# The first output projection in seven half-size products, moved behind gate B's first units, with the modulation paced by half units

## The chip, the cores and the metric

The kernel runs on one core of one Trainium2 chip. Its time is the device time of one execution in microseconds; the times below are the median of three runs, and one more execution was recorded by the hardware profiler. TensorE does the matrix products, VectorE and ScalarE the elementwise work, GpSimd (POOL) and SyncE (SP) here mostly issue transfers.

## The reference

One encoder layer over 512 tokens of width 2048, in single precision:

```python
mod = silu(c) @ w_ada + b_ada                      # shift, scale, gate: twice
h = rms_norm(x, norm1_w) * (1 + sc1) + sh1
qa, ka, va, qb, kb, vb, ga, gb = split(h @ w_in)
ya = global_gqa(rope(norm(qa)), rope(norm(ka)), va)      # 8 heads of 128
yb = neighbourhood_attention(qb, kb, vb, nat_rpb)        # 8 heads of 128
merged = sigmoid(ga) * (ya @ w_oa) + sigmoid(gb) * (yb @ w_ob)
x = x + g1 * (merged @ w_out)
h2 = rms_norm(x, norm2_w) * (1 + sc2) + sh2
x = x + g2 * ((silu(h2 @ w_ffn_gate) * (h2 @ w_ffn_up)) @ w_ffn_down)
return rms_norm(x, final_w)
```

`w_oa` and `w_ob` are 1024 x 2048, `w_out` 2048 x 2048, `w_ffn_gate` and `w_ffn_up` 2048 x 5632.

## The kernel before

**Products.** Each single-precision operand is split into a high half (a copy by ScalarE, rounded, line 163) and a low half (the difference, by VectorE, line 165). `mm3` (lines 183 to 185) makes three products of them: high x high, high x low, low x high. It reads the moving columns interleaved: of each `n` columns, one from the first half, then one from the second. So tokens come out in another order, which the host's `MERGED` and `LAST` undo.

**Units.** Weights come in units of 512 KB: `unit` (line 190) loads a `raw` tile through SP's queue, `wsplit` splits it into one `whl` tile. There are four `raw` and three `whl` buffers; where a pool `wq` is open, `buffer` gives some more of both. `form1` uses a unit's weights as the stationary side against all 512 tokens, 24 products a unit; `form2` streams the weights. After each unit both call `pump`.

**`pump`** is where other work enters the program's order: what is due in `soon`, one entry of `later`, then `pace["steps"]` steps of the generators in `bg`. One of these is the modulation: `ada_acc` adds one 128 x 1024 block of `w_ada`, scaled by `cact`, to `acc` on VectorE (line 357); the block `mw` is fetched through POOL's queue (line 335), three at a time. 112 such steps are done until the end of the output projections, 16 more during `w_out`, from SP's queue. After each 16 steps the sum is split, summed over the partitions by TensorE (`row_sum`, `row_products`) and stored.

**Order.** A scheduler lays out each engine's instructions by their order in the program and by when it expects inputs and buffers to be ready; a modulation step is pinned behind VectorE's instruction traced before it. The order of the stages after global attention (`att_a`):

- `gates(sg_b, GB, 0, 8)`: gate B's first 1024 columns, four calls of `form1` with 4 units each; `keep_gate` applies the sigmoid (line 609) and stores the tiles to memory. Modulation begins here, one step per unit.
- Two halves of neighbourhood attention: values by `form2`, then per pair of heads queries and keys by `form1` and the attention `att_b`. The attended heads are stored as `y_d`, as those of `att_a` were.
- `gates(sg_b, GB, 8, KT)`: gate B's rest, while `attended` loads and splits all 16 heads, one per pump, through SP's queue (lines 816 and 163).
- The output projections: for each pair of column blocks `form1` with `w_oa` on the heads of A, `form1` with `w_ob` on those of B, 2 units each. `gated` loads the gate (line 843; those of A that are still raw get their sigmoid here, line 845) and multiplies (line 847); the two are added (line 859) and split into `mT`. Steps per pump follow a list `paces`.
- `w_out`, residual and norm, then the feed-forward network.

**Seven products.** The feed-forward network's first two matrices use `group7`: both operands are cut into 2 x 2 blocks; with sums of blocks seven block products take the place of eight. `wforms` makes the sums of a weight's blocks on VectorE (lines 1008 to 1011) and splits them into four `whl` tiles, `xforms` does the same for the tokens' side once, and lines 1081 to 1093 put the seven results together. A product has 256 columns there. `wq` gives it one more `raw` and two more `whl`.

Of the kernel before, what the change touches and what calls it, by code (L numbers as in the profile page):

```python
# [54 lines left out]
MERGED = stream_order(T)  # L55
LAST = MERGED[stream_order(T // 2)]

# [55 lines left out]
def encoder_block(ctx: ExitStack, tc, xp, xT, c, ada1_w, ada2_w, b_ada, norm1_w, w_in, q_norm_w, k_norm_w, bias,  # L113
# [13 lines left out]
    wbufs = {"raw": 4, "w": 3, "at": 0}  # L127
    wq = None
    taken = collections.Counter()

    def buffer(tag, shape, dt, first, name=None):

        more = {"raw": 1, "whl": 2}[tag] if wq else 0
# [72 lines left out]
    pace = {"steps": 1}  # L206

    paces = []

    def pump():  # L210
        if paces:
            pace["steps"] = paces.pop(0)
# [6 lines left out]
        for _ in range(pace["steps"]):  # L219
            advance()  # L220

    def advance():
        if bg:
            try:
                next(bg[0])
            except StopIteration:
                bg.pop(0)
                advance()

    def form1(ws, c0, g, xs, banks, evac, eng=V):  # L230
# [3 lines left out]
        for k0 in range(0, n, nk):  # L234
            m = min(nk, n - k0)
            for w, bs in zip(ws, banks):
                hi, lo = wsplit(w, k0, m, c0, g * P, eng)
# [10 lines left out]
    def form2(w, c0, xs, evac, r0=0, eng=V, tiles=range(NT), tags=("mm",) * NT):  # L248
# [3 lines left out]
        for k0 in range(0, n, 2):  # L252
            m = min(2, n - k0)
            hi, lo = wsplit(w, r0 + k0, m, c0, 512, eng)
            for kk in range(m):
                xh, xl = xs[k0 + kk]
                for i in tiles:
                    sl = slice(i * P, (i + 1) * P)
                    mm3(banks[i], xh[:, sl], xl[:, sl], hi[:, kk], lo[:, kk], k0 + kk == 0, k0 + kk == n - 1, 256)
            pump()  # L260
# [297 lines left out]
    for k1 in range(1, KT + 1):  # L558
# [19 lines left out]
        for c0, accs, ends in GROUPS:  # L578
# [8 lines left out]
            for i, acc in enumerate(accs):  # L587
                sl = slice(i * P, (i + 1) * P)
                b = bank(next(turn))
                for k in range(a0, k1):  # L590
# [3 lines left out]
                    else:  # L594
                        mm3(b, wh[:, sl], wl[:, sl], hh, hl, k == a0, k == k1 - 1, T)
# [17 lines left out]
    def gates(dst, base, j0, j1, eng=V):  # L613
        for j in range(j0, j1, 2):
            form1([w_in], base + j * P, 2, hT, [[bank("mm"), bank("mm")]], keep_gate(dst[j:]), eng)


    p_a = tc.alloc_tile_pool(name="p_a", bufs=1, side="right")
    behind(nc.sync.dma_start(rp, rope.rearrange("p (i s d) -> p i s d", i=NT, s=2)))
    nw = {}  # L620
    for nm, w in (("q", q_norm_w), ("k", k_norm_w)):
        nw[nm] = small.tile([P, HD], F32, tag=f"nw{nm}", name=f"nw{nm}", bufs=1)
        nc.sync.dma_start(nw[nm], w.partition_broadcast(P).rearrange("p o d -> p (o d)"))

    def head_ssq(src, nh, acc):
        for h in range(nh):
            junk = io.tile([P, 512], F32, tag="io", name="junk")[:, :HD]
            S.activation(junk, src[:, h * HD:(h + 1) * HD], AF.Square, accum_out=acc[:, h:h + 1])

    def norm_rope(src, nh, i, r, w, dst):  # L630

        n = nh * HD
        h3 = lambda a: a[:, :n].rearrange("p (h d) -> p h d", h=nh)
        bt = lambda a: a.unsqueeze(1).to_broadcast([P, nh, a.shape[1]])
        a, b, rot = (p_a.tile([P, 512], F32, tag="rt", name="rt", bufs=3) for _ in range(3))
        for h in range(nh):
            hs = slice(h * HD, (h + 1) * HD)
            V.scalar_tensor_tensor(b[:, hs], src[:, hs], r[:, h:h + 1], w, op0=ALU.mult, op1=ALU.mult)
        V.tensor_mul(h3(a), h3(b), bt(rp[:, i, 0, :]))
        for e in range(2):  # L640
# [868 lines left out]
```

## Time and profile before

| | |
|---|---|
| runs, median (lowest, highest) | 2486.97 us (2481.64, 2489.78) |
| profiled execution, its own time | 2481.72 us |
| its span, first to last instruction | 2480.0 us |
| TensorE busy | 2449.8 us, 99% |
| VectorE busy | 1883.9 us, 76% |
| ScalarE busy | 1027.6 us, 41% |
| DMA, mean over the span | 184 GB/s |
| `w_oa` and `w_ob` products | 852.7 to 1020.5 us |

In the profile's rows, PE is TensorE, DVE is VectorE, ACT is ScalarE; `mm<-whl,h3h` is a product that writes the buffer `mm` from `whl` and `h3h`, with buffer numbers left out. A row of a group gives shapes, the count, the busy time, the mean of one in ns, and behind the second bar the idle time of its engine just before it, with what ended it. TensorE's instructions overlap, so that the time from start to start is shorter than what one lasts.

### The profile page before, as it was taken

To read this page: it belongs to the slowest core of one execution; us is meant where nothing else is said; L and a number is where in the kernel's file an instruction comes from. 1 tells how busy PE (TensorE), PEld (TensorE's weight loads), DVE (VectorE), ACT (ScalarE), POOL (GpSimd) and SP (SyncE) were. 2 spreads that over 40 slices of the span, in tenths; PEclk is the share of its full clock that TensorE was granted. 3 is DMA by queue.
4 is the path that set the end of the run, shared out by engine and by line. 5 is a ranking of instruction groups with operands and counts; after the bars stand their busy time and mean duration, and the time that the engine had idled before them with its cause. 6 is when DMAs were issued, how large, how long until landed. Compare 5 with 4: busy or idle time off the path is not lost.

```text
span 2480.0 us, 40653 instructions
## 1 busy us (share of the span) xinstructions
PE 2449.8 (99%) x16607; PEld 2270.1 (92%) x16607; DVE 1883.9 (76%) x2511; ACT 1027.6 (41%) x1424; POOL 151.0 (6%) x254
## 2 busy tenths in 40 slices
PE   8999999999999999999999999999999999999998
PEld 7888888888888888888999999999999998999997
DVE  8995776556566577566898888888888885787877
ACT  5223544224334333236744444444444454434333
POOL 0100000111011111011000000000000000000010
PEclk9999999999999999999999999999999999999999
DMA  9864234865655877676353343433433456547563
GB/s 362 296 245 156 81 102 135 273 203 184 191 187 195 300 252 264 233 266 229 111 170 117 122 130 127 136 125 112 132 128 129 135 187 227 190 141 242 192 243 127
DMA packets 217466, 457.46 MB, mean 184 GB/s; under 512 B 15056, under 2 KB 68672, under 8 KB 208832
## 3 DMA queue, kind: packets, MB, share of 16 engines
q1 hardware_dynamic: 179872, 308.19, 37.6%
q0 software_dynamic: 29728, 132.20, 15.2%
q10 hardware_dynamic: 7680, 14.48, 1.6%
q8 instruction: 130, 2.13, 0.3%
q14 instruction: 56, 0.46, 0.1%
HBM read 410.74 MB, written 44.07 MB: 183 GB/s over the span
## 4 chain that ended last, share of the span: by engine, by line
PE 82%; DVE 9%; DMA 4%; issue 2%; ACT 1%; DVEq 0%; POOL 0%; ACTq 0%; POOLq 0%
PE mm L185 18%; PE mm L184 18%; PE mm L183 17%; PE S L183 6%; PE S L184 6%; PE S L185 6%; PE Y L183 3%; PE Y L184 3%; PE Y L185 3%; DVE raw L492 2%; DVE whl L165 2%; DMA raw<-in_w_down 1%; DMA yr<-y 1%; PE T L185 1%; PE T L183 1%
## 5 line engine op out<-in xcount | busy, mean ns | idle before, releaser
L163 ACT ACTIVATE whl<-raw 128x1024 fp32r<-128x1024 f32 (+1 forms) x483 | 462.0, 960 | 758.5 <-PE mm L185 376.5
L165 DVE TENSOR_TENSOR whl<-raw,whl 128x1024 fp32r<-128x1024 f32 (+1 forms) x483 | 531.2, 1109 | 255.5 <-ACT whl L163 255.1
L165 DVE TENSOR_TENSOR whl<-ta,whl 128x1024 fp32r<-128x1024 f32 x104 | 127.2, 1223 | 66.4 <-ACT whl L163 66.4
L357 DVE SCALAR_TENSOR_TENSOR acc<-mw,cact,acc 128x1024 f32<-128x1024 f32 x124 | 158.4, 1278 | 18.8 <-DMA mw<-in_ada_w 14.0
L163 ACT ACTIVATE whl<-tb 128x1024 fp32r<-128x1024 f32 x104 | 110.4, 1061 | 149.6 <-PE S L185 120.1
L163 ACT ACTIVATE whl<-ta 128x1024 fp32r<-128x1024 f32 x104 | 110.1, 1059 | 144.8 <-PE mm L185 113.9
L165 DVE TENSOR_TENSOR whl<-tb,whl 128x1024 fp32r<-128x1024 f32 x104 | 127.0, 1221 | 4.6 <-ACT whl L163 3.6
L335 POOL DMA_DIRECT2D mw<-in_ada_w x112 | 59.8, 534 | 681.7 <-DVE acc L357 384.1
L1008 DVE TENSOR_TENSOR ta<-raw 128x512 f32<-128x512 f32 x104 | 71.8, 690 | 31.5 <-DMA raw<-in_w_down 29.3
L1009 DVE TENSOR_TENSOR ta<-raw,ta 128x512 f32<-128x512 f32 x104 | 71.6, 688 | 28.0 <-DMA raw<-in_w_down 24.9
L183 PE MATMUL mm<-x56h,whl 128*128 128x256 f32 x336 | 92.4, 275 | 0.0
L184 PE MATMUL mm<-x56l,whl 128*128 128x256 f32 x336 | 92.4, 275 | 0.0
L185 PE MATMUL mm<-x56h,whl 128*128 128x256 f32 x336 | 92.4, 275 | 0.0
L183 PE MATMUL mm<-whl,s 128*128 128x256 f32 x320 | 88.1, 275 | 0.0
L183 PE MATMUL mm<-x3h,whl 128*128 128x256 f32 x320 | 88.0, 275 | 0.0
L184 PE MATMUL mm<-x3l,whl 128*128 128x256 f32 x320 | 88.0, 275 | 0.0
L185 PE MATMUL mm<-x3h,whl 128*128 128x256 f32 x320 | 88.0, 275 | 0.0
L183 PE MATMUL S<-x56h,whl 128*128 128x256 f32 x320 | 88.0, 275 | 0.0
L184 PE MATMUL S<-x56l,whl 128*128 128x256 f32 x320 | 88.0, 275 | 0.0
L185 PE MATMUL S<-x56h,whl 128*128 128x256 f32 x320 | 88.0, 275 | 0.0
L184 PE MATMUL mm<-whl,s 128*128 128x256 f32 x320 | 88.0, 275 | 0.0
L185 PE MATMUL mm<-whl,s 128*128 128x256 f32 x320 | 88.0, 275 | 0.0
(1603 smaller groups left out, 8574.4 us busy)
## 6 DMA issues: line engine op xcount, KB each, us to landing
raw<-in_w_in SPq DMA_DIRECT2D x133, 512.0 KB, 4.4
mw<-in_ada_w POOLq DMA_DIRECT2D x112, 512.0 KB, 4.9
raw<-in_w_gate SPq DMA_DIRECT2D x92, 512.0 KB, 3.6
raw<-in_w_up SPq DMA_DIRECT2D x88, 512.0 KB, 3.6
raw<-in_w_down SPq DMA_DIRECT2D x88, 512.0 KB, 5.2
raw<-in_ada_w POOLq DMA_DIRECT2D x29, 1024.0 KB, 7.0
raw<-in_w_out SPq DMA_DIRECT2D x48, 512.0 KB, 5.1
ffd<-c SPq DMA_DIRECT2D x10, 1024.0 KB, 4.8
```

Of the source, the lines that this page charges most:

```text
L163: high = pin(S.activation(hi, src, AF.Copy))
L165: latest[:] = [high, pin(eng.tensor_sub(lo, src, hi))]
L183: nc.tensor.matmul(o, lh, rh, start=start, stop=False, **kw)
L184: nc.tensor.matmul(o, lh, rl, start=False, stop=False, **kw)
L185: nc.tensor.matmul(o, ll, rh, start=False, stop=stop, **kw)
L335: mod["queue"].dma_start(w, ada2_w[n * P:(n + 1) * P, :])
L357: behind(V.scalar_tensor_tensor(acc, part, cact[:, k:k + 1], acc, op0=ALU.mult, op1=ALU.add))
L492: V.scalar_tensor_tensor(raw, raw, 1.0, call, op0=ALU.mult, op1=ALU.mult, accum_out=y)
L1008: V.tensor_sub(t1, b12, b11)
L1009: V.tensor_sub(t2_, b22, t1)
```

## The change

`w_oa` leaves the loop of the output projections. After `att_a` a pool `p_o` is opened as `wq`, with one more `raw` and one more `whl`. Two calls of `form1` for gate B follow; in their pumps `yforms` loads the eight heads of A from memory and makes their seven forms. Then four times `merged_a`: it fetches a quarter of gate A, applies the sigmoid where it is still raw, calls `group7` with `w_oa` (two units, K = 1024), multiplies by the gate and stores the quarter as `ma_d`. After the second and third of them comes one more call of `form1` for gate B each. `group7`, `wforms` and their helpers move up in the file with no other change.

`gates(sg_b, GB, 8, KT)` then reads only B's eight heads. The last loop does `w_ob` alone and loads A's part from `ma_d`.

The modulation's generators go to a list of their own, `mods`. They start with neighbourhood attention, and `slot`, called twice per unit (after half of its products and after `pump`), makes a step when `pace["rate"]` has added up to one: 0.8 in the values, 0.75 in queries and keys, 0.65 in gate B's rest, 0.95 in the first five turns of the `w_ob` loop, none in the last three and in the first pass of `w_out`, then 0.5. `row_products` come after one pump more. All `mm3` outside global attention's scores interleave by 256 columns instead of 512, so that the seven products' order is that of everything they meet.

```diff
-MERGED = stream_order(T)
-LAST = MERGED[stream_order(T // 2)]
+MERGED = stream_order(T // 2)
+LAST = MERGED[MERGED]
...
+    def slot():
+        pace["due"] += pace["rate"]
+        if pace["due"] >= 1 and (fetched or mod["next"] < mod["end"]):
+            pace["due"] -= 1
+            advance(mods)
...
         if later:
             later.pop(0)()
-        for _ in range(pace["steps"]):
-            advance()
+        advance(bg)
+        slot()
...
-                        mm3(bs[j], hi[:, kk, sl], lo[:, kk, sl], xh, xl, k0 + kk == 0, k0 + kk == n - 1, T)
+                        mm3(bs[j], hi[:, kk, sl], lo[:, kk, sl], xh, xl, k0 + kk == 0, k0 + kk == n - 1, 256)
+                    if kk == m // 2 - 1:
+                        slot()
                 pump()
...
-        soon.append((1, lambda: row_products(hl, tag, dst, then)))
+        soon.append((2, lambda: row_products(hl, tag, dst, then)))
...
     p_a.release()
     p_q.release()
+    wq = tc.alloc_tile_pool(name="p_o", bufs=1, side="right", reuse_waits="tile")
+    more_buffers(1, 1)
...
+    def yforms(s):
+        e, o = (raw_tile("ye") for _ in range(2))
+        for a, r in enumerate((e, o)):
+            for q in range(2):
+                nc.sync.dma_start(half(r)[:, :, q], y_d[4 * s + 2 * a + q].rearrange("p (t n) -> p t n", t=2))
...
+        V.tensor_add(sa[:, :512], a21, a22)
+        V.tensor_sub(sa[:, 512:], sa[:, :512], a11)
+        V.tensor_sub(sb[:, :512], a11, a21)
+        V.tensor_sub(sb[:, 512:], a12, sa[:, 512:])
...
+            split(*hl, src)
...
+    def merged_a(n):
+        c, g = (wq.tile([P, 2048], F32, tag=t, name=t, bufs=1) for t in "cg")
+        v, gv = quarters(c), quarters(g)
+        for f in range(4):
+            nc.gpsimd.dma_start(gv[:, f // 2, :, f % 2], sg_a[4 * n + f].rearrange("p (t n) -> p t n", t=2))
+        if n < 3:
+            S.activation(g, g, AF.Sigmoid)
+        group7(lambda s: wforms(w_oa, 4 * s, n * 512), ya, (0, 1), ((v[:, 0, 0], v[:, 1, 0]), (v[:, 0, 1], v[:, 1, 1])))
+        for a in range(2):
+            sl = slice(a * 1024, (a + 1) * 1024)
+            V.tensor_mul(c[:, sl], c[:, sl], g[:, sl])
+        nc.gpsimd.dma_start(ma_d[n], c)
+
+    for s in range(2):
+        later.extend([lambda: None, functools.partial(yforms, s), lambda: None, lambda: None])
+    gates(sg_b, GB, 0, 4)
+    for n in range(4):
+        merged_a(n)
+        if n in (1, 2):
+            gates(sg_b, GB, 2 * n + 2, 2 * n + 4)
+    wq.release()
+    wq = None
+    more_buffers(0, 0)
     p_w = tc.alloc_tile_pool(name="p_w", bufs=1, side="right")
     mod["pool"] = p_w
-    bg.extend(ada_mod(k, (s2, b_sc2, n2, t2, b_sh2)) for k in range(0, KT, 4))
+    mods.extend(ada_mod(k, (s2, b_sc2, n2, t2, b_sh2)) for k in range(0, KT, 4))
...
-    gates(sg_b, GB, 0, 8)
+    fetch()
...
+        pace["rate"] = 0.8
+        form2(w_in, VB + hh * 512, hT, lambda i, b: split(*v[i], b))
+        pace["rate"] = 0.75
...
-    later.extend(functools.partial(attended, h) for h in range(KT))
+    later.extend(functools.partial(attended, h) for h in range(8))
+    pace["rate"] = 0.65
     gates(sg_b, GB, 8, KT)
...
-            if any(src[j] is t for t in sg_a[:12]):
-                S.activation(g, g, AF.Sigmoid)
...
-    paces.extend([2, 1, 1, 1, 1, 1, 1] * 4 + [0] * 4 + [0] * 2 + [1] * 16)
     for j in range(0, KT, 2):
+        pace["rate"] = 0.95 if j < 10 else 0.0
         ma, mb = [], []
-        for w, ys, sg, to in ((w_oa, yT[:8], sg_a, ma), (w_ob, yT[8:], sg_b, mb)):
-            tag = next(turn)
-            form1([w], j * P, 2, ys, [[bank(tag), bank(tag)]], gated(sg[j:], to))
+        for e in range(2):
+            ma.append(p_y.tile([P, T], F32, tag="ma", name="ma", bufs=4))
+            a, q = divmod((j + e) % 4, 2)
+            nc.sync.dma_start(ma[e].rearrange("p (t n) -> p t n", t=2), quarters(ma_d[j // 4])[:, a, :, q])
+        tag = next(turn)
+        form1([w_ob], j * P, 2, yT, [[bank(tag), bank(tag)]], gated(sg_b[j:], mb))
...
     for cc in range(2):
         w_out_pass(cc, range(NT))
+        pace["rate"] = 0.5
```

More of the change, by code (lines that the diff above doesn't have):

```diff
@@ L611, in keep_gate, with gates @@
         return evac
-    def gates(dst, base, j0, j1, eng=V):
+    def gates(dst, base, j0, j1):
         for j in range(j0, j1, 2):
[L615 to L623, printed above, removed]
@@ L810, in encoder_block @@
[L810 to L821 removed]
+            form1([w_in], base + j * P, 2, hT, [[bank("mm"), bank("mm")]], keep_gate(dst[j:]))
     def half(t, n=2):
@@ L866, in encoder_block @@
-    p_y.release()
-    p_w.release()
-    aside.release()
-    taken.update({t: -1 - taken[t] for t in ("raw", "whl")})
-    wq = tc.alloc_tile_pool(name="wq", bufs=1, side="right", reuse_waits="tile")
-    x2_d = dram.tile([T, D], F32, name="x2d")
-    p_w = tc.alloc_tile_pool(name="p_w2", bufs=1, side="left", reuse_waits="tile")
-    mod.update(pool=p_w, queue=nc.sync, end=128)
-    p_r = tc.alloc_tile_pool(name="p_r", bufs=1, side="right", reuse_waits="tile")
-    gate = p_r.tile([P, D], F32, name="gate1")
@@ new lines, in values @@
+    def values():
+        for i in range(NT):
+            v = st(F32R)
+            vA.append((v[:, :256], v[:, 256:]))
+            split(*vA[i], kv[i][:, 256:])
+            if i % 2:
+                yield
+    vA = []
+    q = pair(p_a, "q", 4 * T, 1)
+    bg.extend([normed(kv, 2, nw["k"], kT), normed(q_acc, 4, nw["q"], q), values()])
+    q1 = [st(F32) for _ in range(NT)]
+    form2(w_in, QA + 512, hT, lambda i, b: S.activation(q1[i], b, AF.Copy))
+    flush()
+    y_d = [dram.tile([P, T], F32, name=f"y{h}") for h in range(16)]
@@ new lines, in encoder_block, with attended, __init__, __getitem__ @@
+    p_b.release()
+    p_y = tc.alloc_tile_pool(name="p_y", bufs=1, side="right", reuse_waits="tile")
+    yT = [pair(p_y, f"y{k}", T, 1) for k in range(8)]
+    def attended(h):
+        yr = raw_tile("yr")[:, :T]
+        nc.sync.dma_start(yr, y_d[8 + h])
+        split(*yT[h], yr)
+    later.extend(functools.partial(attended, h) for h in range(8))
+    pace["rate"] = 0.65
+    gates(sg_b, GB, 8, KT)
+    p_h.release()
+    class Tokens:
+        def __init__(self, t):
+            self.t = t
+        def __getitem__(self, ix):
+            t, c = divmod(ix[1].start // P, 2)
+            return self.t[:, t, c * P:(c + 1) * P]
@@ new lines, in encoder_block, with gated, evac @@
+    p_m = tc.alloc_tile_pool(name="p_m", bufs=1, side="left")
+    mx = [pair(p_m, f"m{j}", 1024, 1) for j in range(KT // 2)]
+    mT = [tuple(Tokens(half(t)[:, :, k % 2]) for t in mx[k // 2]) for k in range(KT)]
+    def gated(src, dst):
+        def evac(w, j, b):
+            g = io.tile([P, T], F32, tag="io", name="g")
+            nc.sync.dma_start(g, src[j])
+            o = p_y.tile([P, T], F32, tag="o", name="o", bufs=4)
+            V.tensor_mul(o, g, b)
+            dst.append(o)
+        return evac
@@ new lines, in encoder_block @@
+    p_y.release()
+    p_w.release()
+    aside.release()
+    more_buffers(1, 2)
+    wq = tc.alloc_tile_pool(name="wq", bufs=1, side="right", reuse_waits="tile")
+    x2_d = dram.tile([T, D], F32, name="x2d")
+    p_w = tc.alloc_tile_pool(name="p_w2", bufs=1, side="left", reuse_waits="tile")
+    mod.update(pool=p_w, queue=nc.sync, end=128)
+    p_r = tc.alloc_tile_pool(name="p_r", bufs=1, side="right", reuse_waits="tile")
+    gate = p_r.tile([P, D], F32, name="gate1")
+    xc = {cc: p_r.tile([P, NT, 512], F32, tag=f"x{cc}", name=f"x{cc}") for cc in (3, 2)}
@@ new lines, in encoder_block, with load_x @@
+    xn = [None, None, xc[2], p_r.tile([P, NT, 512], F32, tag="n3", name="n3")]
+    xc.update({cc: p_r.tile([P, NT, 512], F32, tag=f"x{cc}", name=f"x{cc}") for cc in (0, 1)})
+    xn[:2] = xc[0], xc[1]
+    sq2 = [small.tile([P, 4], F32, tag=f"sq{i}", name=f"sq{i}", bufs=1) for i in range(NT)]
+    x3d = xp.rearrange("(i p) d -> p i d", p=P)
+    def load_x(cc):
+        if cc == 0:
+            rows(gate, g1_d)
+        nc.sync.dma_start(xc[cc], x3d[:, :, cc * 512:(cc + 1) * 512])
+    for cc in range(4):
+        later.extend([lambda: None] * (2 if cc == 0 else 3))
+        later.append(functools.partial(load_x, cc))
```

541 lines of the change are left out of this document (253 added, 288 removed).

## The prediction

> **What bounds the kernel now.** I read the page's totals and chain first, then the table of stretches, then the waits of the stages that the change touches, last the rows that carry a duration.
>
> ```profile
> span 2480.0 us, 40653 instructions
> PE 2449.8 (99%) x16607; PEld 2270.1 (92%) x16607; DVE 1883.9 (76%) x2511; ACT 1027.6 (41%) x1424; POOL 151.0 (6%) x254
> PE 82%; DVE 9%; DMA 4%; issue 2%; ACT 1%; DVEq 0%; POOL 0%; ACTq 0%; POOLq 0%
> ```
>
> TensorE is busy for 99% of the span and makes up 82% of the chain of waits. So time goes away only where TensorE gets fewer products, or where it now stands idle. The table of stretches shows both (columns: stretch, length, busy us and count by engine, granted clock, DMA share, GB/s). The first five rows are the stages: gate B's first four units with the end of attention A, neighbourhood attention, gate B's last units, the two output projections, and the start of `w_out`.
>
> ```profile
> 400.00:480.00 80.00, 79.68 (x390) 68.39 (x389) 44.25 (x49) 25.50 (x36) 11.12 (x21) 1.00 0.75 254
> 480.00:780.00 300.00, 298.90 (x1481) 256.61 (x1480) 182.64 (x257) 108.11 (x198) 34.29 (x61) 1.00 0.57 182
> 780.00:853.00 73.00, 71.31 (x328) 61.42 (x328) 49.45 (x53) 28.59 (x38) 13.59 (x24) 1.00 0.94 326
> 853.00:1020.00 167.00, 167.00 (x775) 146.12 (x774) 113.61 (x128) 49.74 (x61) 18.93 (x35) 1.00 0.71 240
> 1020.00:1120.00 100.00, 100.00 (x465) 87.49 (x464) 61.64 (x60) 30.99 (x43) 15.21 (x13) 1.00 0.80 272
> 880.00:980.00 100.00, 100.00 (x465) 87.50 (x464) 78.22 (x86) 29.94 (x38) 14.87 (x29) 1.00 0.83 284
> 1250.00:2000.00 750.00, 750.00 (x6719) 750.00 (x6718) 647.80 (x807) 331.31 (x351) 0.00 (x0) 1.00 0.40 128
> 780.00:800.00 20.00, 20.00 (x94) 17.46 (x94) 14.55 (x16) 8.48 (x12) 5.16 (x9) 1.00 0.98 344
> ```
>
> TensorE's idle time from 400 to 1120 us is 0.32 + 1.10 + 1.69 = 3.1 us. That is all that a better order of the work can win there.
>
> **The products of w_oa.** One wide and one narrow product last:
>
> ```profile
> L183 PE MATMUL mm<-whl,a 128*128 128x512 f32 x48 | 18.2, 379 | 0.0
> L183 PE MATMUL mm<-x56h,whl 128*128 128x256 f32 x336 | 92.4, 275 | 0.0
> ```
>
> They overlap, so I count starts. Between 880 and 980 us TensorE runs 512-column products only. 465 of them touch the 100 us, some 463 begin there: 0.216 us from start to start. From 1250 to 2000 us it runs the feed-forward network's 256-column products: 6719 touch 750 us, 0.1117 us each. Before, `w_oa` takes 8 k-blocks x 16 column blocks x 3 = 384 wide products, 384 x 0.216 = 82.9 us. After, it takes 4 groups x 2 units x 7 products x 4 pieces x 3 = 672 narrow ones, 672 x 0.1117 = 75.1 us. **Gain 7.9 us**, not the 10.4 us that an eighth of 82.9 would be, since two narrow products take 0.223 us against 0.216.
>
> The Trainium skill (TensorE: Matmul & The Clock Gate, Back-to-back issue gap) gives an isolated warm product N / 2.4 + 2.5 ns: 215.8 for 512 columns, 109.2 for 256. The wide rows agree; for the narrow ones the trace has 111.7 and decides. By the rule the gain would be 9.5 us.
>
> All other products stay: interleaving tokens over 256 instead of 512 changes addresses, not counts, and the feed-forward rows already use that form. I take 0 for it.
>
> **Gate B's last units, 780 to 853 us.** TensorE loses 1.69 us here. It waits for split weights:
>
> ```profile
> PE mm L185 <- DVE whl L165: 1.6, 2, 0.9
> ```
>
> The split that ended the first of these waits, and ScalarE's queue in front of it:
>
> ```profile
> 819.83 1.22 DVE L165 TENSOR_TENSOR whl<-raw,whl 128x1024 fp32r<-128x1024 f32 x1
> ```
>
> ```profile
> 816.12 0.63 ACT L845 ACTIVATE g<-g 128x512 f32<-128x512 f32 x1 [3.23 <-DMA g<-sga]
> 822.16 0.63 ACT L845 ACTIVATE g<-g 128x512 f32<-128x512 f32 x1 [2.73 <-DMA g<-sga]
> 823.43 0.63 ACT L163 ACTIVATE y12h<-yr 128x512 fp32r<-128x512 f32 x1 [0.65 <-DMA yr<-y]
> ```
>
> ScalarE stands before gate A's sigmoid and before attended heads, whose loads are late at a DMA share of 0.94; the weight's high half is queued behind. The change removes both from this queue: gate A is not loaded here, and 8 heads are read instead of 16. Against that the modulation rises from one step per unit to 1.3. In bytes per unit of 24 x 0.216 = 5.18 us: half a head less, 0.13 MB, and 0.3 steps of 512 KB more, 0.16 MB. So DMA stays as full, but ScalarE no longer waits at its head for sigmoid loads. Bounds 0 and -1.7; I take **-1.4 us**.
>
> **Where modulation starts.** Its first fetch waits for memory of the pool before it:
>
> ```profile
> DVE acc L355 <- DMA mw<-in_ada_w: 7.0, 1, 7.0
> ```
>
> ```profile
> 419.28 0.75 DVE L355 TENSOR_SCALAR acc<-mw,cact 128x1024 f32<-128x1024 f32 x1 [7.00 <-DMA mw<-in_ada_w]
> ...
> 425.35 1.29 DVE L357 SCALAR_TENSOR_TENSOR acc<-mw,cact,acc 128x1024 f32<-128x1024 f32 x1 [1.01 <-DMA mw<-in_ada_w]
> 426.56 1.22 DVE L165 TENSOR_TENSOR whl<-raw,whl 128x1024 fp32r<-128x1024 f32 x1
> ```
>
> VectorE stands 7 us, and the next weight split comes behind four steps, at 426.56; TensorE loses 0.32 us in that stretch. This leaves the first stage (-0.3) and returns at neighbourhood attention. There the memory is that of the new pool, whose last user is the 1 MB store of a merged group: a load of that size lands in 4.8 us.
>
> ```profile
> ffd<-c SPq DMA_DIRECT2D x10, 1024.0 KB, 4.8
> ```
>
> The wait may grow to 12 us, but weights have three buffers, two 5.18 us units ahead. Bounds 0 and +2; **+0.5**.
>
> **The new stage.** Attention A's heads are read and split there, and VectorE makes sums. Its durations from the same code in the feed-forward network:
>
> ```profile
> L165 DVE TENSOR_TENSOR whl<-ta,whl 128x1024 fp32r<-128x1024 f32 x81 | 99.1, 1224 | 58.3 <-ACT whl L163 58.3
> L165 DVE TENSOR_TENSOR whl<-tb,whl 128x1024 fp32r<-128x1024 f32 x81 | 98.9, 1221 | 0.9
> L1008 DVE TENSOR_TENSOR ta<-raw 128x512 f32<-128x512 f32 x82 | 56.6, 690 | 2.1
> L1182 DVE TENSOR_TENSOR c<-c 128x1024 f32<-128x1024 f32 x20 | 23.5, 1220 | 0.0
> L1083 DVE TENSOR_TENSOR c<-mm,p 128x512 f32<-128x512 f32 x19 | 13.1, 692 | 21.6 <-PE mm L185 21.6
> ```
>
> A unit costs VectorE four sums (2.8), a half split (0.7, a sum's width) and three full ones (3.7): 7.1 us. A group is two units, seven sums of products (4.8) and two multiplications (2.4): 21.4 us. TensorE needs 168 x 0.1117 = 18.8 us for it. So a group alone is VectorE's by 2.6 us. But gates lie between: four calls of four units, 20.7 us each of TensorE against four splits, 4.9 us, of VectorE. The stage has 158 us of TensorE and 4 x 21.4 + 4 x 4.9 + 14 for the heads' forms = 119 us of VectorE, no modulation. Only the first two groups stand back to back, and the forms of their first unit are made during the gates. In the feed-forward network VectorE has 647.8 of 750 us and TensorE waits for nothing. Bounds 0 and 4 x 2.6 = 10.4; nearest is the feed-forward row; **+0.5**. ScalarE's wide sigmoids and the copies of the first product lie beside this (it has 41% of the span); ScalarE holds nothing up that TensorE waits for. SP issues 8 head loads between weight loads, POOL 16 quarter gates and 4 stores, while no modulation fetch is on POOL; row sums that come one pump later have no reader near.
>
> **Neighbourhood attention** gets 73 steps (by counting slots: 25 in the values, 48 in queries and keys) instead of 46.
>
> ```profile
> L357 DVE SCALAR_TENSOR_TENSOR acc<-mw,cact,acc 128x1024 f32<-128x1024 f32 x46 | 58.7, 1276 | 0.0
> ```
>
> ```profile
> L335 POOL DMA_DIRECT2D mw<-in_ada_w x112: 527/528/641, 412.6 to 975.8; - x112
> DMA to landing us min/median/max: 3.1/4.9/8.9
> ```
>
> 27 x 1.28 = 35 us more of VectorE in 300, from 183 to 217, and 14 MB more, from 182 to 229 GB/s: both have room. POOL issues each fetch in 0.53 us. What is queued behind a step is the next split, which its three buffers let run up to two units ahead. **+0.3 us** (0 to 1.1, a doubling of the idle time there).
>
> **The w_ob loop** is the tightest place. Eighteen steps fall into its first ten units, 1.8 per unit. Rows of the stage today:
>
> ```profile
> L165 DVE TENSOR_TENSOR whl<-raw,whl 128x1024 fp32r<-128x1024 f32 x32 | 39.1, 1221 | 37.4 <-ACT whl L163 37.4
> L847 DVE TENSOR_TENSOR o<-g,mm 128x512 f32<-128x512 f32 x21 | 13.7, 683 | 9.2 <-PE mm L185 9.2
> L859 DVE TENSOR_TENSOR o<-o 128x512 f32<-128x512 f32 x14 | 9.0, 685 | 0.0
> ...
> L165 DVE TENSOR_TENSOR m5l<-o,m5h 128x512 fp32r<-128x512 f32 x2 | 1.3, 686 | 0.0
> ```
>
> ```profile
> mw<-in_ada_w POOLq DMA_DIRECT2D x26, 512.0 KB, 5.7
> raw<-in_w_ob SPq DMA_DIRECT2D x14, 512.0 KB, 4.2
> ...
> g<-sgb SPq DMA_DIRECT2D x15, 256.0 KB, 4.9
> ```
>
> Per unit: split 1.22, product by gate 0.68, sum 0.69, low half 0.69, modulation 1.8 x 1.28 = 2.30: 5.58 us of VectorE against 5.18. Over ten units it falls back 4 us. Per unit DMA brings 0.52 MB of weights, two tiles of 0.26, and 1.5 fetches (three are there already) of 0.52: 1.83 MB, 354 GB/s, where the row at 780 shows 344 at a share of 0.98. What covers this: splits lead by up to two units, and ScalarE loses the sigmoid loads that today hold weights back (the 37.4 above). Low bound 0 (this stretch has no idle now at 284 GB/s), high bound 4.5 (1.83 MB at the 326 GB/s of 780 to 853 takes 5.63 us, ten times 0.45); **+1.5**. Then `w_out`: one slot left over makes a step in its first unit, fifteen more follow from the second pass. Some fall on half-size units of 2.6 us, where split and step take 2.5. Five weight buffers cover eight such units: 0 (0 to 2).
>
> **The sum:** -7.9 - 1.4 - 0.3 + 0.5 + 0.5 + 0.3 + 1.5 = **-6.8 us**. The profiled execution took 2481.72 us (span 2480.0 and 1.7 around it), which is the low edge of the runs (2481.64 to 2489.78). The three runs and it have a mean of 2485.0; 6.8 off that is 2478.2, off the median 2480.2. I predict **2479.2 us**.
>
> **Rivals.** *The w_ob loop is paced by memory:* steps wait for fetches, splits stand behind the steps, TensorE pays 4.5 plus VectorE's 1 to 2 that lead doesn't cover. For it: 354 over 344. Against: 0.83 share costs nothing now. It gives 2479.2 + 4.5 = 2484. The Trainium skill (DMA: Bandwidth & Descriptors, Specifications) has about 358 GB/s from HBM per core; by that the loop would just fit.
>
> *All idle goes:* none of the small terms comes and all 1.7 us at gate B's end return: -7.9 - 1.7 - 0.3 = -9.9, 2476. Against it: VectorE's 5.58.
>
> *The new stage starves TensorE (slower):* four weight buffers, not the five of the feed-forward network, and sums of a finished group queued on VectorE ahead of the next unit's forms. Then each group pays its 2.6 us and the start of its forms, four sums and a half split, 3.5: 4 x 6.1 = 24 us, 2503. It decides once forms come less than 3.5 us before their use. Against: gates of 20.7 us between groups.
>
> *It doesn't do what it says:* were narrow products no cheaper in sum, nothing would be left; 6719 of them say otherwise. No chance of its own.
>
> **Chances.** A measurement here tells 0.3%, 7.5 us, from no change. Forecast 0.46 (2475 to 2482; a little over half of it is faster by more than 0.3%), all idle goes 0.18 (faster), memory paces 0.23 (within), starved 0.12 (slower), rest 0.01. So faster 0.44, same 0.43, slower 0.13. Range 2472 to 2490: below for all idle gone and the spread of runs, above for memory pacing with a stall in the new stage; the starved case is left out.
>
> **What would show it.** Right: some 384 fewer 512-column products and 672 more narrow ones between 400 and 570 us without idle TensorE; the stretch of gate B's last units without its 1.7 us. Wrong: waits of TensorE for `whl` in the w_ob loop with VectorE standing for `mw`, or in the groups of the new stage with VectorE full. The prediction fails if either exceeds 5 us.

## The result and the profile after

The changed kernel is slower: 2517.65 us at the median of six runs (2509.90 to 2522.36), against 2485.26 for the kernel before (2481.64 to 2489.78, six runs). The ratio is 1.0129, 95% interval 1.0109 to 1.0149. The forecast of 2479.2 us and its range up to 2490 were wrong, on the wrong side. One run of all that are told of here, of e9 below, took 9090.1 us; without it e9's median is 2481.21 us and not 2481.27, and why it took so long isn't known.

The totals of the changed kernel's profiled execution, whose own time is 2509.90 us, the lowest of its runs:

```profile
span 2508.0 us, 41404 instructions
PE 2451.8 (98%) x16895; PEld 2276.0 (91%) x16895; DVE 1945.2 (78%) x2587; ACT 1044.7 (42%) x1435; POOL 165.4 (7%) x274
```

TensorE has 288 more instructions (672 - 384), as forecast. The span is 28 us longer: TensorE is idle for 26 us more (56.2 against 30.2) and busy for 2 us more (2451.8 against 2449.8), though its products should take 7.9 us less. The table of stretches says where (columns as in the prediction; the third number from the end is the granted clock):

```profile
395.00:420.00 25.00, 16.49 (x86) 12.64 (x85) 19.36 (x32) 16.08 (x26) 2.88 (x4) 0.86 0.48 146
420.00:480.00 60.00, 60.00 (x416) 56.43 (x415) 42.96 (x52) 26.10 (x29) 2.68 (x4) 1.00 0.48 157
480.00:575.00 95.00, 93.06 (x618) 86.17 (x618) 60.28 (x71) 33.06 (x35) 8.07 (x12) 1.00 0.53 179
600.00:640.00 40.00, 32.64 (x142) 27.97 (x141) 27.15 (x27) 8.94 (x14) 7.41 (x14) 0.91 0.86 284
870.00:955.00 85.00, 80.39 (x381) 68.10 (x380) 56.46 (x68) 30.05 (x47) 17.65 (x31) 1.00 0.87 309
955.00:1040.00 85.00, 81.33 (x369) 70.47 (x368) 64.90 (x77) 26.32 (x34) 7.86 (x15) 0.98 0.81 265
```

These are, in order: the end of attention A; the first two groups of seven products; the other two with gate B's units between them; the end of the first values of neighbourhood attention; gate B's rest; the `w_ob` loop. TensorE is idle for 8.5, 0, 1.9, 7.4, 4.6 and 3.7 us in them, 26.1 in all; another 3.5 us lie between 640 and 870 us. Three of the rows have a granted clock below 1: an estimate from these rows of what this cost the products is 0.14 x 25 + 0.09 x 40 + 0.02 x 85 = 8.8 us. With it the busy time comes out: -7.9 + 8.8 = +0.9, near the +2.0 measured. What TensorE waited for from 380 to 1040 us (in total, times, longest):

```profile
PE mm L187 <- DVE vl L169: 8.0, 2, 7.4
PE mm L187 <- ACT whl L167: 6.5, 2, 5.2
PE mm L189 <- DVE whl L169: 4.0, 5, 2.3
PE S L189 <- DVE whl L169: 3.7, 1, 3.7
PE S L188 <- DVE kl L169: 2.1, 3, 1.6
PE mm L187 <- ACT go L625: 1.6, 1, 1.6
```

**The end of attention A.** SP's queue in the kernel before, and then in the changed kernel (start, how long the issues span, what, how many):

```profile
331.31 96.86 SPq L190 DMA_DIRECT2D raw<-in_w_in  x10
```

```profile
330.33 0.37 SPq L194 DMA_DIRECT2D raw<-in_w_in  x1
348.10 4.39 SPq L893 DMA_DIRECT2D ye<-y  x4
356.13 55.99 SPq L194 DMA_DIRECT2D raw<-in_w_in  x4
```

The last line joins loads that lie far apart. Two of its four are issued by 361.7 us:

```profile
356.13 5.55 SPq L194 DMA_DIRECT2D raw<-in_w_in  x2
```

The heads of A are loaded at 348 us, while attention A still runs, and into the `raw` buffers that weights use. Their sums can be made only when attention A's memory is free. VectorE and ScalarE there:

```profile
409.23 0.69 DVE L897 TENSOR_TENSOR sa<-ye 128x512 f32<-128x512 f32 x1 [1.58 <-PE Y L189]
```

```profile
413.33 4.10 ACT L167 ACTIVATE whl<-raw 128x1024 fp32r<-128x1024 f32 x4
```

The two `ye` tiles wait from 348 to 409 us for the last products of attention A (`PE Y`). From 330 to 412 us the weights of gate B get five loads. Two of those weights are issued by 361.7 us and yet are split only at 413.33: ScalarE has the splits of the heads ahead of them. So attention A's last steps, short products with softmax between them, run with no products of gate B to fill the gaps: 86 products in the first of the stretches. Then TensorE waits 5.2 us for the first weight. The heads thus hold gate B up in two ways: they keep buffers, and they stand ahead of its splits. No run separates the two: e1 below puts a weight ahead of the heads in both.

**The first values.** POOL, VectorE and ScalarE of the changed kernel:

```profile
572.85 0.56 POOL L920 DMA_DIRECT2D mad<-c  x1 [28.50 <-DVE c L919]
577.78 1.59 POOL L351 DMA_DIRECT2D mw<-in_ada_w  x3 [4.37 <-DMA mad<-c]
```

```profile
584.36 0.75 DVE L371 TENSOR_SCALAR acc<-mw,cact 128x1024 f32<-128x1024 f32 x1 [3.68 <-DMA mw<-in_ada_w]
...
608.79 1.28 DVE L373 SCALAR_TENSOR_TENSOR acc<-mw,cact,acc 128x1024 f32<-128x1024 f32 x1 [2.49 <-DMA mw<-in_ada_w]
...
614.78 1.28 DVE L373 SCALAR_TENSOR_TENSOR acc<-mw,cact,acc 128x1024 f32<-128x1024 f32 x1
615.98 2.48 DVE L169 TENSOR_TENSOR vl<-mm,vh 128x512 fp32r<-128x512 f32 x4
```

```profile
607.45 2.54 ACT L167 ACTIVATE vh<-mm 128x512 fp32r<-128x512 f32 x4 [2.18 <-PE mm L189]
```

The last group's store lands, the first three blocks are fetched, and the first step runs at 584.36. The program's order wants 0.8 steps per half unit of 2.6 us, one in 3.2 us, from the first unit on; here they come late, in a row, and wait for their blocks. The four values leave ScalarE at 607.45, but on VectorE their low halves stand behind the steps that are not done yet, and start at 615.98. They hold four result banks, so TensorE cannot begin the next products: 7.4 us.

### The profile page after: what moved, and what is told of

It is laid out like the page before. It is cut to its first block, busy times and chain, and to the rows that moved or that the text cites. A ratio compares the mean times of both kernels' runs of the same rounds, so it can differ in the third digit from the quotient of the medians.

```text
span 2508.0 us, 41404 instructions
## 1 busy us (share of the span) xinstructions
PE 2451.8 (98%) x16895; PEld 2276.0 (91%) x16895; DVE 1945.2 (78%) x2587; ACT 1044.7 (42%) x1435; POOL 165.4 (7%) x274
## 4 chain that ended last, share of the span: by engine, by line
PE 75%; DVE 11%; issue 7%; DMA 4%; ACT 1%; POOL 1%; SPq 0%; DVEq 0%; POOLq 0%; ACTq 0%
PE mm L187 15%; PE mm L188 15%; PE mm L189 15%; PE S L189 5%; PE S L187 5%; PE S L188 5%; PE Y L187 3%; PE Y L188 3%; PE Y L189 3%; DVE raw L508 3%; DVE whl L169 2%; DMA mw<-in_ada_w 2%; DVE acc L373 1%; PE T L189 1%; PE T L188 1%
## 5 line engine op out<-in xcount | busy, mean ns | idle before, releaser
L169 DVE TENSOR_TENSOR whl<-ta,whl 128x1024 fp32r<-128x1024 f32 x112 | 137.2, 1225 | 88.0 <-ACT whl L167 88.0
L167 ACT ACTIVATE whl<-ta 128x1024 fp32r<-128x1024 f32 x112 | 118.5, 1058 | 159.1 <-PE mm L189 120.6
L167 ACT ACTIVATE whl<-tb 128x1024 fp32r<-128x1024 f32 x112 | 118.7, 1060 | 158.2 <-PE S L189 122.1
L169 DVE TENSOR_TENSOR whl<-tb,whl 128x1024 fp32r<-128x1024 f32 x112 | 136.8, 1222 | 17.0 <-ACT whl L167 15.9
L678 DVE TENSOR_TENSOR ta<-raw 128x512 f32<-128x512 f32 x112 | 77.4, 691 | 37.7 <-DMA raw<-in_w_down 25.1
L679 DVE TENSOR_TENSOR ta<-raw,ta 128x512 f32<-128x512 f32 x112 | 77.2, 690 | 29.4 <-DMA raw<-in_w_down 24.2
```

Of the source, the lines that this page charges most:

```text
L167: high = pin(S.activation(hi, src, AF.Copy))
L169: latest[:] = [high, pin(eng.tensor_sub(lo, src, hi))]
L678: V.tensor_sub(t1, b12, b11)
L679: V.tensor_sub(t2_, b22, t1)
```

## The experiments

In all diffs the left side is the changed kernel, or the one that is named. "Before" is run beside each; on these chips it took 2487 to 2489 us.

### Head forms later (e1)

```diff
-        later.extend([lambda: None, functools.partial(yforms, s), lambda: None, lambda: None])
+        later.extend([lambda: None] * (4 if s == 0 else 1) + [functools.partial(yforms, s)])
+    later.append(lambda: None)
```

> The changed kernel with the forms of A's heads three pumps later: the first after the fifth unit of gate B, the second after the seventh. Theory 'held buffers': the two head loads take two of the four raw weight buffers from 348 us on and cannot give them back before attention A ends, so gate B's units cannot be split during attention A and TensorE has nothing to fill that attention's waits with (about 15 us of idle and slowed products between 390 and 420 us against some 3 before). Then TensorE's products from gate B go on through attention A, the stretch from 395 to 420 us gets back most of its 8.5 us of TensorE idle time, and the time falls by 8 to 13 us, to about 2507 us. Rival 'the new pool's memory': what gate B's units wait for is the extra weight buffers laid over attention A's memory; then later forms change nothing: 2514 to 2521 us.

2504.82 us (2502.06 to 2509.33), ratio 1.0072 (1.0057 to 1.0087): 12.8 us less than the changed kernel. The same stretch and the first wait of this kernel:

```profile
395.00:420.00 25.00, 24.32 (x137) 19.87 (x136) 18.68 (x31) 16.41 (x27) 2.88 (x4) 1.00 0.44 136
```

```profile
PE mm L187 <- DVE vl L169: 8.8, 1, 8.8
```

The idle time of attention A's end goes from 8.5 to 0.7 us, and the granted clock from 0.86 to 1.00; by these rows that is 7.8 and 3.5 us of the 12.8. The wait for the values stays. SP's and ScalarE's queues of e1 show that not only the buffers matter:

```profile
356.15 7.45 SPq L893 DMA_DIRECT2D ye<-y  x4
```

```profile
365.07 1.05 ACT L167 ACTIVATE whl<-raw 128x1024 fp32r<-128x1024 f32 x1
```

Two `ye` tiles are still loaded early here and first read at 407.87 us, so they stand full for over 50 us, and the idle time is gone even so. What is new is that a weight of gate B is split at 365.07, before attention A's last steps, where the changed kernel splits none until 413.33. So held buffers alone don't make this loss; the order on ScalarE and VectorE counts as well.

### First values without steps (e2)

```diff
-        pace["rate"] = 0.8
+        pace["rate"] = 0.8 if hh else 0.0
...
-        pace["rate"] = 0.75
+        pace["rate"] = 0.95
```

> The changed kernel with no modulation step in the first half's values and 0.95 instead of 0.75 per slot in queries and keys, the same number of steps in all. Theory 'steps ahead of the values' split': the 7.4 us wait of TensorE at the end of the first values comes from modulation steps that stand on VectorE ahead of the split of the values, late because their first fetch waits for the memory of the pool before. Then that wait goes, queries and keys pay 1 to 3 us more, and the time falls by 6 to 10 us, to about 2510 us. Rival 'too many steps wherever they are': the same wait appears at the next split from a bank, of queries or keys: 2514 to 2521 us.

2502.37 us (2499.82 to 2505.22), ratio 1.0061 (1.0046 to 1.0076): 15.3 us less than the changed kernel, more than expected. The wait for `vl` falls from 8.0 to 0.3 us. The steps return elsewhere in part: the waits for `kl` rise from 2.1 to 4.1 us in all, and one of 2.4 us for the split of a row sum appears. Of the gain only 4.6 us stands between the two profiled executions (spans 2508.0 and 2503.4): the changed kernel's is the lowest of its six runs, e2's the highest of its own.

### The new pacing in the kernel before (e3)

`w_oa` stays as it was; only `mods`, `slot`, the later start and row products that come one pump later come in, with a rate of 0.475 in the loop, which has twice the units:

```diff
+    gates(sg_b, GB, 0, 8)
     p_w = tc.alloc_tile_pool(name="p_w", bufs=1, side="right")
...
-    bg.extend(ada_mod(k, (s2, b_sc2, n2, t2, b_sh2)) for k in range(0, KT, 4))
+    mods.extend(ada_mod(k, (s2, b_sc2, n2, t2, b_sh2)) for k in range(0, KT, 4))
...
-    gates(sg_b, GB, 0, 8)
+    fetch()
```

> The kernel before with the new pacing alone: modulation by slots of half units, from neighbourhood attention on, with the rates of the change, and half the rate in the loop of the output projections, which is twice as long here (w_oa stays in it with its 384 wide products). Theory 'two separate losses': the pacing costs what the changed kernel shows from 600 us on, 9 at the values, 3 at gate B's rest, 2 elsewhere, and perhaps nothing in the longer loop: 2496 to 2503 us. Rival 'the pacing is harmless and the new stage's memory and order make it late': within 4 us of the kernel before, 2481 to 2490 us.

2497.24 us (2494.45 to 2498.47), ratio 1.0038 (1.0023 to 1.0053). The pacing loses 10 us by itself. But its largest wait is another one, at gate B's rest (831 us), where the products of a row sum wait in TensorE's order for a split:

```profile
PE T L382 <- ACT acch L163: 5.5, 1, 5.5
PE S L184 <- DVE kl L165: 2.8, 3, 2.3
```

The wait for `vl` is 0.2 us here, though the values have the same rate of 0.8 and the same three `mw` buffers. The difference is when the first blocks are fetched and so how soon `vl` gets its turn on VectorE:

```profile
412.94 1.08 POOL L343 DMA_DIRECT2D mw<-in_ada_w  x2 [251.30 <-PE Y L185]
```

```profile
519.39 2.63 DVE L165 TENSOR_TENSOR vl<-mm,vh 128x512 fp32r<-128x512 f32 x4 [0.36 <-ACT vh L163]
```

The blocks are asked for long before the first values, the steps ahead of the low halves aren't late, and these follow ScalarE within 0.36 us.

### No modulation (e4, e6)

120 of the 128 steps are left out, so that the modulation's sums are not computed: once in the changed kernel, once with the late head forms.

```diff
-            fetch()
-            part = fetched.popleft()
...
+            if k == 0:
+                part = mod["pool"].tile([P, 1024], F32, tag="mw", name="mw", bufs=3)
+                mod["queue"].dma_start(part, ada2_w[mod["next"] * P:(mod["next"] + 1) * P, :])
...
+            mod["next"] += 1
```

> The changed kernel with 120 of the 128 modulation steps left out: of each sum only the first block is fetched and scaled, so modulation comes out incomplete; slots, row sums and everything else stay. Theory 'two separate losses': what is left is the gain of 7.9 us in products, the loss of some 11 us at the end of attention A and 2 in the new stage, less the idle time that modulation costs in either kernel (3 us before): 2485 + 11 + 2 - 7.9 - 3 = 2487, between 2482 and 2494 us. Rival 'modulation is the whole of it': 2474 to 2479 us. Rival 'the new stage itself is slow': above 2495 us.

2491.23 us (2484.16 to 2492.59), ratio 1.0011 (1.0001 to 1.0022).

> The kernel with late head forms, with 120 of the 128 modulation steps left out (only the first block of each sum is fetched and scaled). Both losses that were found are then away. Theory: 2491 for the changed kernel without modulation less the 12.4 us of late head forms, 2478 to 2481 us, which is the kernel before less the 7.9 us of products. Rival 'the new stage eats the gain': 2484 to 2490 us.

2480.95 us (2477.17 to 2484.41), ratio 0.9966 (0.9954 to 0.9978). Without any modulation, the early head forms still cost 10.3 us (2491.23 against 2480.95): the two losses have separate causes. I first read the 7.4 us to the kernel before as the products' gain. That was wrong, as the next runs show.

### The kernel before without modulation (e9, e11, e12)

The text of e9 names a wrong count: here too 120 of the 128 steps are left out.

> The kernel before with 104 of its 112 + 16 modulation steps' worth of fetches and sums left out in the same way as in the two runs without modulation (only the first step of each sixteen is done, so the modulation sums are wrong). It tells what the 7.4 us are by which the late kernel without modulation was under the kernel before. Theory (seven products gain about 7.5 us, and the kernel before hides its modulation): 2485 to 2488 us, the same as the kernel before. Rival (the modulation costs the kernel before several microseconds, and the late kernel without it was faster only for lacking it, the products giving little): 2479 to 2483 us.

2481.27 us, ratio 0.9967 (0.9954 to 0.9979). This is the rival: the kernel before pays for its modulation as well, 7.9 us at the median. So e6 had gained nothing that could be seen. The pair was then run on one chip:

> The kernel before without its modulation steps (120 of the 128 are left out, the first of each sixteen stays; the modulation sums are wrong), next to the late kernel without them on one chip and in one set of rounds: apart they came out equal, 0.9967 and 0.9966 of the kernel before. Theory (seven products save 7.8 us of TensorE's time, the new stage gives 4 us of it back in short waits that the profiles show between 400 and 520 us): this one 2480 to 2483 us, the late one 2 to 5 us below it. Rival (nothing of the saving arrives): the two within 1.5 us. Rival (all of it arrives and the earlier equality was the chips): 6 to 8 us between them.

> The late kernel without its modulation steps (120 of the 128 are left out; the sums are wrong), the other of the pair. Theory (saving less the new stage's waits): 2 to 5 us below the kernel before without modulation. Rival (nothing arrives): within 1.5 us of it. Rival (all arrives): 6 to 8 us below it.

2480.97 us (ratio 0.9975, 0.9965 to 0.9986) for the kernel before without modulation, 2477.95 (0.9958, 0.9944 to 0.9971) for the late one: 3.0 us between the medians. The theory's 2 to 5 is met by the medians, while the intervals overlap. The profiles show one part of what is missing from the 7.9. From 395 to 575 us, first the kernel before without modulation, then the late one, then the late one's waits from 380 to 1120:

```profile
395.00:575.00 180.00, 180.00 (x880) 156.19 (x881) 67.32 (x97) 60.37 (x90) 5.80 (x10) 1.00 0.41 128
```

```profile
395.00:575.00 180.00, 176.75 (x1167) 161.85 (x1166) 124.24 (x159) 76.25 (x93) 15.22 (x23) 1.00 0.53 177
```

```profile
PE mm L187 <- ACT go L626: 1.7, 1, 1.7
...
PE mm L189 <- DVE whl L169: 0.9, 1, 0.9
```

The late kernel idles 3.25 us where the old order idles 0: 0.68 of it before 420 us, at attention A's end, and 2.57 in the new stage. That would leave 7.9 - 3.25 = 4.6 us, but over the whole span the two profiles show no gain: 2478.5 and 2479.0 us. TensorE is busy for 2448.4 and 2444.2 us, which is 4.2 less and not 7.9, and idle for 4.7 more. The late one's profiled execution is among the longest of its runs, so this doesn't settle it either. How much of the 7.9 arrives isn't shown; 3.0 us at the median is the best figure here. The largest of the stage's waits is for `go`, and ScalarE's queue of the late one tells why:

```profile
499.51 1.91 ACT L916 ACTIVATE g<-g 128x2048 f32<-128x2048 f32 x1 [10.21 <-DMA g<-sga]
...
502.28 0.57 ACT L626 ACTIVATE go<-mm 128x512 f32<-128x512 f32 x1
```

ScalarE stands 10.21 us before the sigmoid of a quarter of gate A, whose load isn't there. Behind it wait a weight's split and the two copies that free gate B's banks, and a group needs seven banks.

### An earlier first fetch (e5)

Late head forms, and the modulation's pool waits for single tiles of the pool before it, not for all of it:

```diff
-    p_w = tc.alloc_tile_pool(name="p_w", bufs=1, side="right")
+    p_w = tc.alloc_tile_pool(name="p_w", bufs=1, side="right", reuse_waits="tile")
```

> The kernel with late head forms (2504.8 us), and the modulation's pool waiting for each tile it lies over instead of for the whole pool before it; VectorE's order of instructions is the same. Theory 'late start': the steps ahead of the first values' split are late because their first fetch waits for the last store of the new stage, some 6 us after the values begin. Then the fetch leaves 4 to 8 us earlier, the 8.8 us wait of TensorE for the values' split falls below 4, and the time to 2496 to 2501 us. Rival 'fetch rate': fifteen steps in the 41 us of the values need one fetch in 2.7 us, three in flight, and come late however early they begin: 2502 to 2507 us.

2502.02 us (2497.94 to 2508.52), ratio 1.0055 (1.0035 to 1.0075), against 2504.82 in e1. The first block is asked for right behind the store, but the next two only 4.1 us later, and the longest wait for `vl` is still 5.6 us (8.8 in e1). The intervals of the two ratios overlap, so a gain isn't clear. Only part of the late start is gone, and only part of the wait. The rate of the fetches, three in flight, isn't enough by itself to make the wait: e3 has the same rate and the same three buffers, but its first blocks come some 60 us ahead, and it waits 0.2 us. What fits e1, e3 and e5 is that the late start makes the backlog, and that three buffers can't make it up before the values' evacuation. A run with a fourth `mw` buffer wasn't made.

### Late forms and quiet values (e8), an even spread (e7), evacuation first (e10)

e8 has the edits of e1 and e2 together.

> Late head forms and quiet first values together. If the two losses are separate places they add: 2517.65 - 12.8 - 15.3 = 2489.5 us, 2486 to 2493. If they share a cause (slack handed from one to the other), less: 2495 to 2502 us.

2491.71 us (2487.82 to 2498.85), ratio 1.0018 (1.0005 to 1.0031). They take 25.9 us off the changed kernel, one by one 12.8 and 15.3: they add up but for 2 us. This is the best version with modulation, and not faster than the kernel before.

e7 has the late forms, no steps in the first values, lower rates up to `w_out` but for queries and keys (0.8 for 0.75), and 32 steps instead of 16 in `w_out`:

```diff
-    mod = {"pool": None, "queue": nc.gpsimd, "next": 0, "end": 112}
+    mod = {"pool": None, "queue": nc.gpsimd, "next": 0, "end": 96}
...
+        pace["rate"] = 0.6 if hh else 0.0
...
+        pace["rate"] = 0.8
...
+    pace["rate"] = 0.55
...
+        pace["rate"] = 0.9 if j < 10 else 0.0
...
+    pace["rate"] = 0.625
...
+        pace["rate"] = 0.375
```

> Late head forms; 96 modulation steps instead of 112 before w_out and 32 in it; none in the first values, 0.8 per slot in queries and keys, 0.6 in the second values, 0.55 in gate B's rest, 0.9 in five turns of the w_ob loop, 0.625 and 0.375 in w_out. Theory 'density': fewer steps per unit of every stage that lost time leave TensorE waiting less than 8 us for modulation in all: 2479 to 2486 us, at or below the kernel before. Rival 'the order, not the density': steps pinned ahead of the splits of keys and gates cost 10 us or more wherever they are: 2488 to 2496 us.

2502.28 us (2498.21 to 2503.24), ratio 1.0050 (1.0035 to 1.0065): a miss for both. The idle time of neighbourhood attention (575 to 870 us) shrank from 10.9 us in the changed kernel to 3.1, the `w_ob` loop still loses 4.4, and `w_out` took on another loss:

```profile
1100.00:1200.00 100.00, 93.31 (x426) 79.32 (x426) 76.94 (x87) 56.55 (x85) 16.26 (x13) 0.97 0.76 249
```

6.7 us are idle from 1100 to 1200, with no wait over 1.9 us. e10 is e8 with the last half step and pump of a product put behind its evacuation (the same in `form2`):

```diff
-                    if kk == m // 2 - 1:
+                    if kk == m // 2 - 1 and k0 + m < n:
                         slot()
-                pump()
+                if k0 + m < n:
+                    pump()
         for wi, bs in enumerate(banks):
             for j in range(g):
                 evac(wi, j, bs[j])
+        for _ in ws:
+            slot()
+            pump()
```

> The kernel with late head forms and quiet first values, with one thing more: the half step and the pump of a product's last weight unit come after the product's evacuation in the program's order, so that modulation steps pinned behind it no longer stand ahead of the splits of queries, keys, values and of the gates' products. Theory (what is left of the loss is mostly the order on VectorE ahead of evacuations, like the 3.5 us wait for the keys' split): 2486 to 2490 us, the wait for kl gone. Rival (the steps' fetches and the weight splits behind them keep their cost wherever the steps stand): 2490 to 2496 us.

2497.83 us (2493.68 to 2501.91), ratio 1.0032 (1.0020 to 1.0045). The intervals of e8 and e10 overlap, so whether it is worse isn't settled; better it is not. The waits of e8, then of e10 (both up to 1180 us):

```profile
PE S L188 <- DVE kl L169: 3.5, 1, 3.5
PE mm L187 <- ACT whl L167: 3.3, 3, 2.0
```

```profile
PE mm L187 <- ACT whl L167: 4.5, 5, 2.7
...
PE T L397 <- DVE accl L169: 2.0, 1, 2.0
PE T L397 <- ACT acch L167: 1.9, 1, 1.9
```

The wait for `kl` is gone, as wanted, and its time came back as waits for weights and for the splits of a row sum. That is the rival's case.

## Why the prediction was wrong, step by step

**Where the 32 us come from**, by the runs. The early head forms cost 10.3 us (e4 to e6) to 12.8 (e1). The steps in the first values cost 15.3 (e2; 13.1 from e1 to e8). What remains above the kernel before is 3.3 us (e8). If the products with their stage give the -3.0 of e11 and e12, modulation costs some 6 us more in the later stages than it did before; that is a remainder, which no run measures. 12.8 + 13.1 + 3.3 is the way from the changed kernel over e1 and e8 to e8's kernel before (2488.4 us), so it must add up to that distance, 29.3 us. Beside its own runs of before, on another chip, the changed kernel lies 32.4 us over; the 3 us between are not explained.

**The products, -7.9: right in the price of one; the sum isn't shown.** Narrow products of a group follow each other as in the feed-forward network. In the late kernel without modulation the 1st and the 57th of a row of them start (56 x 0.1118 us apart):

```profile
504.79 0.28 PE L188 MATMUL mm<-y05l,whl 128*128 128x256 f32 x1
...
511.05 0.28 PE L187 MATMUL mm<-y12h,whl 128*128 128x256 f32 x1
```

How much of the 7.9 us reaches the end of the kernel stays open (e11, e12).

**The granted clock: not in the sum, some +8.8 us.** I took TensorE's busy time to fall by what the products save. It rose by 2.0 us, since the products ran at a granted clock of 0.86, 0.91 and 0.98 in three of the stretches; by the estimate above that costs 8.8 us. The long wait in each of them is one of the next points, so part of what e1 and e2 win is this.

**The new stage, +0.5: too small, 2.6 in e12, 1.9 in the changed kernel.** I had VectorE's sums as its danger; they cost 0.9 us at most (`whl` from VectorE). The sentence that failed is "ScalarE holds nothing up that TensorE waits for": the sigmoid on a late load stood at the head of ScalarE's queue, the very pattern that I had read in the profile of before and taken as removed. The rival with a starved stage, 24 us, was far off.

**The first stage, -0.3: the largest thing overlooked, +10 to +13.** I counted the eight head loads as issues between weight loads. I didn't ask how long each tile keeps a buffer, nor what stands behind the heads' splits. Two of the `raw` tiles stood full for 61 us, waiting for memory that attention A still used, and two of gate B's weights, asked for by 361.7 us, stood unsplit behind the heads. That the early forms cost the time is shown by e1 and by e4 with e6; which of the two ways it goes is not, and e1, with two tiles full for 52 us and no idle time, speaks for the second. And I named no work that fills attention A's gaps, though in the kernel before it was gate B's products.

**The start of modulation, +0.5 with bounds 0 and +2: +13 to +15 with the steps behind it.** "The wait may grow to 12 us" was right: the last multiplication ends at 572.5, the first step starts at 584.4. But the cover that I named, three weight buffers, covers only the next weight split. Behind the same steps stood the evacuation of four banks, which has no lead at all: the banks are needed at once. The step that failed is that only a weight's split stands behind a late step. I took it here with "weights have three buffers", and said it in the part on neighbourhood attention: "what is queued behind a step is the next split". It failed there for `kl` as well (2.1 us).

**Gate B's last units, -1.4: wrong sign, +3.** TensorE idles 4.6 us in the stretch, 1.69 before. ScalarE in the changed kernel:

```profile
903.26 1.06 ACT L167 ACTIVATE whl<-raw 128x1024 fp32r<-128x1024 f32 x1 [6.93 <-DMA raw<-in_w_in]
```

The sigmoids left this queue, as I said; the weight itself was now late, at a DMA share of 0.87 over the stretch and 0.92 (323 GB/s) from 880 to 920 us. I had equal bytes and drew from it that nothing else would become late. The loads in this stretch tell more (KB each, median us to landing):

```profile
raw<-in_w_in SPq DMA_DIRECT2D x12, 512.0 KB, 8.9
mw<-in_ada_w SPq DMA_DIRECT2D x3, 512.0 KB, 11.2
ma<-mad SPq DMA_DIRECT2D x4, 256.0 KB, 3.8
```

The same weights of the kernel before, from 780 to 853 us:

```profile
raw<-in_w_in SPq DMA_DIRECT2D x11, 512.0 KB, 5.5
```

A weight lands in 8.9 us instead of 5.5. And I had left loads out: the first three blocks for `w_out`'s steps and the first tiles of A's part are asked for here, on SP's queue with the weights, and the eight heads come in the first eight of sixteen units, where I had spread them over all. That these loads make the weights late is argued; no run took them out.

**The `w_ob` loop, +1.5 with bounds 0 and 4.5: the right place and bounds, 3.7.** But not paced by memory (0.81). VectorE:

```profile
966.36 1.28 DVE L373 SCALAR_TENSOR_TENSOR acc<-mw,cact,acc 128x1024 f32<-128x1024 f32 x1
...
991.84 0.68 DVE L169 TENSOR_TENSOR accl<-acc,acch 128x512 fp32r<-128x512 f32 x1
992.44 1.28 DVE L373 SCALAR_TENSOR_TENSOR acc<-mw,cact,acc 128x1024 f32<-128x1024 f32 x1
...
1014.91 1.20 DVE L169 TENSOR_TENSOR whl<-raw,whl 128x1024 fp32r<-128x1024 f32 x1
```

For 25 us no step runs, since the steps keep their order behind the split of a row sum; then eleven begin within 25 us (992.44 to 1017.3), and a weight's split is late. My 5.58 us per unit was a mean over ten units; the work came in a burst. Row sums were the point that I passed over with "no reader near". Whether the one pump more makes that split late wasn't tried.

**`w_out`, 0:** right. From 1040 to 1270 us TensorE is busy for 230.00 us at a granted clock of 1.00. The other products, also taken at 0, are right too: 465 of the wide ones touch the 100 us from 1040, as many as in 100 us before. Once more steps go to `w_out` it is no longer so (e7).

**What bounds the kernel now.** "That is all that a better order of the work can win", 3.1 us, was read from an execution at the low edge of the runs. Without modulation the kernel before gains 7.9 and 8.2 us at the median (e9, e11), while its profile shows only some 2 us less idle time from 400 to 1120 us. Where the median execution loses the rest, no profile here shows.

My sign of failure, over 5 us in the loop or in the groups, did not come. The losses were in stages for which I had named no limit.

## What to carry to other kernels

When work moves past a stage, list for each tile of it how long it holds a buffer, and whose loads and splits stand behind it; and ask what filled the gaps of the stage that now runs alone. Steps that wait for a fetch may stand ahead of a weight's split, which has lead, but not ahead of the evacuation of a result bank, which has none; or their first fetches must come well ahead of them, as in e3. Measure a gain against a kernel that lacks the same thing: here the two kernels without modulation differed by 3 us, where the comparison with the full kernel before had shown 7.4.

## What was not expected of the hardware

In the changed kernel the granted clock is lowest where TensorE's idle time is in one piece: 0.86 in the 25 us with the 5.2 us wait, 0.91 in the 40 us with the 7.4 us wait, 0.98 in the 85 us with the one of 3.7 us, and 1.00 in the 85 us that lose 4.6 us in several waits, the longest of 2.3. So a long wait brings slower products with it, which I had priced nowhere. The Trainium skill (TensorE: Matmul & The Clock Gate, HAM oscillation) has the rule for it: idle gaps over some 3.4 us let the clock drop to half. These four rows agree with it, but other runs don't: in e3 the clock is 0.91 in 20 us whose single wait is 2.3 us, for `kl`, and e7's row from 1100 to 1200 us has 0.97 with no wait over 1.9.

```profile
700.00:720.00 20.00, 17.65 (x87) 15.19 (x86) 17.17 (x27) 6.55 (x14) 4.77 (x9) 0.91 0.83 274
```

So a shorter wait can lower the clock as well, and what decides it isn't shown. Whether the clock is why e2 gained 15.3 us at the median for a wait of 7.4 isn't shown either.

The runs of a kernel spread unevenly: e3's four over 4.0 us, the changed kernel's six over 12.5, with no cause shown. One profiled execution can lie anywhere in that: the changed kernel's is the lowest of its runs, e2's the highest.
